# A pool mixer that projects before it pools, more expert tiles transposed ahead, and another order of their loads

## The chip, the cores and the metric

One NeuronCore of a Trainium2 chip runs the whole program. The metric is device time in microseconds (us). TensorE is PE (its weight loads are PEld), VectorE is DVE, ScalarE is ACT, GpSimd is POOL and SyncE is SP. All DMAs of this kernel but the row gathers are issued from SP's queue, in order.

## The reference

The input is `x`, 512 tokens of 1024 features, fp32. Two blocks follow one another.

The first block is a pool mixer with a residual and a layer norm. Cut to what matters:

```
h = x @ w_in;  u, z = split(h)                    # 2048 columns each
for g, w in enumerate((2, 4, 8, 16)):             # 4 groups of 512 columns
    m[g] = (sum of the last w rows of u[g]) / min(t + 1, w) - u[g]
    m[g] = (m[g] @ w_grp[g]) * scale[g]
x = layer_norm(2**0.25 * x + (m * silu(z)) @ w_out)
```

Pooling runs along the tokens, and the projection `w_in` along the features, so either may come first.

The second block has a modulation vector `ada = silu(c) @ w_ada`, a mixer of short convolutions and a linear recurrence (LRU), and PEER, a mixture of 16384 experts: each token picks 8 x 16 experts by key scores, and the result is the sum of `coef * expert_v[i]` with `coef = g * gelu(expert_u[i] . h)`.

## The kernel before, in words

**Precision.** Matrices are split into a high and a low fp32r part (`split`, L107: ACT copies the high part, DVE or POOL subtracts for the low one). A product is three matmuls (`mm3`, L137). `wload` (L121) loads 512 KB of weights into a ring of three buffers and splits them.

**Pool mixer (0 to some 375 us).** `x` is transposed on PE, split into `xh` and `xl`, and POOL adds the two back to `xT` (L209). For each of four groups, `x_group` (L232) pools the columns of `xT` on DVE by doubling steps (L239), subtracts (L243), mends the first tokens (L245, L246) and splits the result; `m_group` (L250) projects it with `w_in` (4 x 8 x 3 matmuls of 512 columns); `z_group` (L217) projects `xh`, `xl` for the gate; `gate_group` (L263) applies `w_grp`, scale and gate; `y_group` (L311) applies `w_out` and adds into `ya`. The last group's tail is `last_group` (L281), in which a tile of 128 tokens goes on to the layer norm as soon as it is done. Beside that, `ada` (L334) computes the modulation on DVE from 96 loads of 256 KB, and `ada_fin` (L345) sums it over partitions on PE. The list `AF_` says at which point of a group that is done.

**Convolutions and LRU (375 to 612 us).** 20 weight tiles; between them `pre_u` (L541) transposes tiles of `expert_u` ahead of time: one tile of 128 experts is loaded in two halves, each by four DMAs (`u_load`, L531: one for each quarter of the features, into a strip of 32 partitions), each half is transposed on DVE (L539) and stored to DRAM (`ut_d`, L551). `NU` = 20 tiles are made so, one after each of 16 chunks and four at the end.

**PEER.** The first 128 tokens take their experts by row gathers (L1180, POOL's queue), the other 384 take all 128 tiles of 128 experts densely. `stage_a` (L869) brings tile i of `expert_u` into transposed form and multiplies it with the tokens (24 matmuls of 384 columns):

- i below `NU`: load the finished transpose (L890), split (L893, L894);
- i from `NU` to 37: load the plain tile, transpose it on PE (8 transposes, L881), split out of PSUM (L883, L885);
- i from 38 on: `u_load` in quarters of 128 KB into the ring of weight buffers, transpose on DVE (2 us, L539), split.

Tiles up to 37 run before the dense loop, most of them among the G stage (750 to 951 us), in which one-hot products (L1134) turn the chosen experts into a dense matrix. In the dense loop (some 960 to 1990 us, 128 steps) step i multiplies `expert_v` tile i (`stage_v`, L922) and makes `stage_a(i + 11)`; from step 27 on the gathers run at about 2.5 of 512 KB a step, spread by step number (L1214), and DVE consumes them (L1192, L1203).

The order on each engine and queue is set by the framework's planner (L1290): it lists what is ready by its own model, in the order of the program where it has a choice, so loads and DVE work of a later line can come before waiting work of an earlier one.

## Time and profile before

| | us |
|---|---|
| median of 3 runs (lowest, highest) | 2038.66 (2033.51, 2040.03) |
| the profiled execution: its own time | 2042.83 |
| its span, first to last instruction | 2041.0 |
| PE busy in it | 1822.1 |
| DVE busy in it | 1787.4 |

The page of the profile gives busy time by engine, the span in slices, and the chain of waits that ended last. The view by stretches gives the same for any stage; the groups by line give what each kind of instruction took and what its engine waited for before it; the DMA view gives packets, bytes and the time that packets took. A busy PE is not PE at its peak, since the ends of matmuls are modelled.

### The profile page before, as it was taken

Reading aid. Unit: us, or ns where it says so; the run is one execution under the profiler, and the core shown is the slowest. Engines: PE = TensorE matmul, PEld = TensorE weight load, DVE = VectorE, ACT = ScalarE, POOL = GpSimd, SP = SyncE. Lnnn points to the kernel's source line nnn. Section 1 sums busy time; section 2 is a strip of 40 time slices with the busy share of each in tenths; the row PEclk is TensorE's granted clock in tenths of the full one; section 3 lists DMA queues with packets and bytes.
Section 4 is the critical chain, followed back from the end, with each engine's and each line's share of the span. In section 5 each row is a group of like instructions: output and inputs, shape, how many; then the busy total and the mean of one; then the engine's idle time right before and its main releaser. Section 6 shows DMA issues by size and latency. Waiting matters only on the chain.

```text
span 2041.0 us, 26681 instructions
## 1 busy us (share of the span) xinstructions
PE 1822.1 (89%) x9003; PEld 1586.7 (78%) x9003; DVE 1787.4 (88%) x3088; ACT 827.9 (41%) x1318; POOL 727.3 (36%) x492
## 2 busy tenths in 40 slices
PE   8999889887899968888988899899898998989897
PEld 6787667765699968888777788788787887878886
DVE  8989887989869999896998898899898898989856
ACT  4433333445453359987333232233232232232334
POOL 3113222333340000000245555455555565656424
PEclk9999999998899979999999899999999999999999
DMA  5545583565463325547869999999999999999932
GB/s 166 181 150 151 167 267 107 150 211 178 146 188 97 103 65 207 191 160 251 265 225 288 265 295 262 291 282 291 274 278 276 300 284 282 298 263 293 286 116 97
DMA packets 288293, 441.13 MB, mean 216 GB/s; under 512 B 24600, under 2 KB 203652, under 8 KB 285084
## 3 DMA queue, kind: packets, MB, share of 16 engines
q1 hardware_dynamic: 251292, 305.19, 49.6%
q0 software_dynamic: 36864, 134.23, 21.3%
q8 instruction: 71, 1.16, 0.3%
q14 instruction: 66, 0.54, 0.1%
HBM read 393.11 MB, written 46.23 MB: 215 GB/s over the span
## 4 chain that ended last, share of the span: by engine, by line
DVE 33%; DMA 24%; PE 17%; issue 13%; ACT 5%; POOL 4%; SPq 2%; DVEq 0%; POOLq 0%; ACTq 0%
DMA uraw<-in_expert_u 10%; DMA wraw<-in_expert_v 4%; DMA gu<-in_expert_u,idx 3%; PE bank L140 3%; PE bank L139 3%; PE bank L138 3%; DMA araw<-in_w_ada 2%; DVE wlo L116 2%; DVE ut L539 2%; DVE og L1132 2%; DMA gv<-in_expert_v,idx 2%; DVE junk L1192 2%; DVE sw L239 2%; SPq L534 2%; DVE acc L1203 2%
## 5 line engine op out<-in xcount | busy, mean ns | idle before, releaser
L114 POOL TENSOR_TENSOR wlo<-wraw,whi 128x1024 fp32r<-128x1024 f32 x111 | 290.0, 2614 | 818.3 <-ACT whi L112 799.3
L140 PE MATMUL aux<-h2h,ul 128*128 128x384 f32 x1024 | 368.1, 360 | 75.3 <-DVE ul L116 68.2
L112 ACT ACTIVATE whi<-wraw 128x1024 fp32r<-128x1024 f32 x218 | 229.3, 1055 | 507.3 <-DMA wraw<-in_expert_v 369.4
L138 PE MATMUL aux<-h2h,uh 128*128 128x384 f32 x1024 | 363.9, 355 | 14.8 <-ACT gl L904 5.9
L139 PE MATMUL aux<-h2l,uh 128*128 128x384 f32 x1024 | 360.2, 352 | 0.0
L139 PE MATMUL o<-wlo,wh 128*128 128x512 f32 x756 | 298.1, 394 | 11.0 <-DVE wlo L116 10.6
L138 PE MATMUL o<-whi,wh 128*128 128x512 f32 x756 | 291.3, 394 | 9.5 <-ACT whi L112 9.5
L140 PE MATMUL o<-whi,wl 128*128 128x512 f32 x756 | 296.6, 392 | 0.0
L140 PEld LDWEIGHTS aux<-h2h,ul 128*128 128x128 f32 x1024 | 203.8, 199 | 92.4 <-DVE ul L116 83.8
L539 DVE STREAM_TRANSPOSE ut<-uraw 128x1024 f32<-128x1024 f32 x90 | 195.9, 2176 | 71.1 <-DMA uraw<-in_expert_u 70.1
L1180 POOL DMA_INDIRECT gu<-in_expert_u,idx x128 | 173.9, 1359 | 204.6 <-DVE junk L1192 173.3
L1180 POOL DMA_INDIRECT gv<-in_expert_v,idx x128 | 182.8, 1428 | 153.2 <-DVE acc L1203 111.9
L138 PEld LDWEIGHTS aux<-h2h,uh 128*128 128x128 f32 x1024 | 204.4, 200 | 22.7 <-ACT uh L112 7.9
L139 PEld LDWEIGHTS aux<-h2l,uh 128*128 128x128 f32 x1024 | 203.6, 199 | 3.3
L112 ACT ACTIVATE uh<-ut 128x1024 fp32r<-128x1024 f32 x90 | 94.9, 1054 | 205.1 <-DVE ut L539 193.6
L1192 DVE SCALAR_TENSOR_TENSOR junk<-gu,hrow 128x1024 bf16<-128x1024 f32 x128 | 171.8, 1342 | 5.7 <-DMA gu<-in_expert_u,idx 5.6
L1203 DVE SCALAR_TENSOR_TENSOR acc<-gv,cf,acc 128x1024 f32<-128x1024 f32 x127 | 171.3, 1349 | 5.3 <-DMA gv<-in_expert_v,idx 4.9
L139 PEld LDWEIGHTS o<-wlo,wh 128*128 128x128 f32 x756 | 143.3, 190 | 42.1 <-DVE wlo L116 14.0
L138 PEld LDWEIGHTS o<-whi,wh 128*128 128x128 f32 x756 | 143.3, 190 | 37.1 <-ACT whi L112 10.2
L140 PEld LDWEIGHTS o<-whi,wl 128*128 128x128 f32 x756 | 143.4, 190 | 30.2
L116 DVE TENSOR_TENSOR wlo<-wraw,whi 128x1024 fp32r<-128x1024 f32 x107 | 147.9, 1383 | 7.0 <-ACT whi L112 7.0
L138 PE MATMUL bank<-ah,whi 128*128 128x512 f32 (+1 forms) x320 | 123.0, 389 | 6.0 <-ACT ah L112 4.9
(376 smaller groups left out, 3562.5 us busy)
## 6 DMA issues: line engine op xcount, KB each, us to landing
wraw<-in_expert_v SPq DMA_DIRECT2D x128, 512.0 KB
uraw<-in_expert_u SPq DMA_DIRECT2D x360, 128.0 KB
araw<-in_w_ada SPq DMA_DIRECT2D x96, 256.0 KB
g_d<-gs SPq DMA_DIRECT2D x24, 1024.0 KB
gt<-g_d SPq DMA_DIRECT2D x15, 1536.0 KB
wraw<-in_pool_w_in SPq DMA_DIRECT2D x32, 512.0 KB
wraw<-in_w_in SPq DMA_DIRECT2D x20, 512.0 KB
praw<-in_expert_u SPq DMA_DIRECT2D x160, 64.0 KB
```

The source lines that it names most:

```text
L112: S.activation(hi, src, AF.Copy)
L114: G.tensor_tensor(lo, src, hi.bitcast(F32), op=OP.subtract)
L116: V.tensor_tensor(lo, src, hi.bitcast(F32), op=OP.subtract)
L138: i = PE.matmul(out, lhsT=l[0], rhs=r[0], start=first, stop=False)
L139: PE.matmul(out, lhsT=l[0], rhs=r[1], start=False, stop=False)
L140: PE.matmul(out, lhsT=l[1], rhs=r[0], start=False, stop=last)
L239: V.tensor_tensor(nxt[:, :, step:], cur[:, :, step:], cur[:, :, :T - step], op=OP.add)
L534: nc.sync.dma_start(raw[32 * q:32 * q + 32], U[i * P + a0 * 32:i * P + (a0 + na) * 32, q * 256:(q + 1) * 256].rearrange("(a r) d -> r a d" ...
L539: V.transpose(out=ut.rearrange("p k (a r) -> p a k r", r=32), in_=raw.rearrange("p a (c k) -> p a k c", k=KD))
L1180: G.indirect_dma_start(out=r, out_offset=None, in_=src, in_offset=bass.IndirectOffsetOnAxis(ap=idx[t][:, s:s + 1], axis=0))
L1192: paced(V.scalar_tensor_tensor(junk, r, 1.0, hrow[t], op0=OP.mult, op1=OP.mult, accum_out=cf[t][:, s:s + 1]))
L1203: paced(V.scalar_tensor_tensor(acc[t], r, cf[t][:, s:s + 1], acc[t], op0=OP.mult, op1=OP.add))
```

## The change

- The pool mixer projects first. `u_group` computes `u = x @ w_in` for a group with tokens on partitions (4 banks of PSUM, 4 weight loads, 96 matmuls of 512 columns, as `m_group` had), and ACT and DVE split it. `pooled` then pools on PE: for each of 4 column blocks and 4 token tiles it multiplies `u` with a banded matrix of 128 columns and with the 16 columns that reach in from the token tile before; 1/w is applied as the result leaves PSUM. `bands` builds the matrices once. `x_group`, `m_group` and `xT` go.
- The order is u(g+1), gate(g), z(g+1), pooled(g+1), y(g). `AF_` is now (1, 1, 1).
- `NU` is 56. `pre_u` comes three tiles at a time at three points of a group and one after each of the four rows of `y_group`'s second half: 39 tiles in the pool mixer. After each of the 16 chunks of the convolution stage it makes one more, and one at the end.
- `u_load` issues the quarters in the order 0, 2, 1, 3, for the tiles made ahead and for those of the dense loop.
- So in `stage_a` tiles 20 to 55 load the finished transpose; 56 to 127 go on as before.

```diff
-AF_ = (1, 1, 0, 0)
+AF_ = (1, 1, 1)
-NU = 20
+NU = 56
+NP1 = 3
+BW = P + 16
...
-    for q in range(4):
-        G.tensor_tensor(xT[:, 2 * q:2 * q + 2, :], xh[:, q].bitcast(F32), xl[:, q].bitcast(F32), op=OP.add)
...
+    def bands():
+        wide = xp.tile([P, BW], F32, name="wide")
+        past = xp.tile([P, BW], F32, name="past")
+        G.iota(wide, pattern=[[1, BW]], base=0, channel_multiplier=-1, allow_small_or_imprecise_dtypes=True)
+        V.tensor_scalar(past, wide, 0.0, None, op0=OP.is_ge)
+        for g, w_ in enumerate(WINDOWS):
...
+            V.scalar_tensor_tensor(f, wide, float(w_), past, op0=OP.is_lt, op1=OP.mult)
+            V.scalar_tensor_tensor(f[:, :P], ident, -float(w_), f[:, :P], op0=OP.mult, op1=OP.add)
...
+    def u_group(g):
+
+        bs = [bank() for _ in range(NT)]
+        for kk in range(4):
+            w = wload(w_in[kk * 256:(kk + 1) * 256, g * 512:(g + 1) * 512].rearrange("(k p) c -> p k c", p=P), 2)
+            for t in range(NT):
+                s = slice(t * P, (t + 1) * P)
+                for j in range(2):
+                    x = at(xhl, 2 * kk + j)
+                    mm3(bs[t], (x[0][:, s], x[1][:, s]), (w[0][:, j], w[1][:, j]), kk + j == 0, kk == 3 and j == 1)
...
+        for t in range(NT):
+            split(uh[t // 2][:, t % 2], ul[t // 2][:, t % 2], bs[t])
+        return uh, ul
+
+    def pooled(g, u):
...
+            for t in range(NT):
+                m = (band if t else first)[:, :P]
+                o = b[:, t * P:(t + 1) * P]
+                e = o[:, :16]
+                PE.matmul(o, lhsT=part(t, 0), rhs=m, start=True, stop=False)
+                if t == 0:
+                    PE.matmul(e, lhsT=part(t, 0), rhs=rest, start=False, stop=False)
+                else:
+                    PE.matmul(e, lhsT=part(t - 1, 0), rhs=band[:, P:], start=False, stop=False)
+                    PE.matmul(e, lhsT=part(t - 1, 1), rhs=band[:, P:], start=False, stop=False)
+                PE.matmul(o, lhsT=part(t, 1), rhs=m, start=False, stop=True)
...
+            S.activation(h, b, AF.Copy, scale=1.0 / WINDOWS[g])
+            V.scalar_tensor_tensor(l, b, 1.0 / WINDOWS[g], h.bitcast(F32), op0=OP.mult, op1=OP.subtract)
...
     def u_load(raw, i, a0, na):
 
-        for q in range(4):
+        for q in (0, 2, 1, 3):
             nc.sync.dma_start(raw[32 * q:32 * q + 32],
...
+    u = u_group(0)
     sz = z_group(0)
+    bands()
...
-    xg = act_tiles()
-    list(x_group(0, xg))
...
-    for g in range(4):
-        mhl = m_group(g, xg)
...
+    mhl = pooled(0, u)
+    for g in range(3):
+        pre_u(NP1)
+        u = u_group(g + 1)
+        pre_u(NP1)
         ghl = gate_group(g, mhl, sz)
         if AF_[g] == 1:
             ada_fins()
-        xg = act_tiles()
-        sz = z_group(g + 1, x_group(g + 1, xg))
+        sz = z_group(g + 1)
+        pre_u(NP1)
+        mhl = pooled(g + 1, u)
...
         for _ in y_group(g, ghl):
-            pass
+            pre_u(1)
+    ada_fins()
     p1.close()
```

## Rows read from the trace of the kernel before

**Rows 1.** The page: the chain that ended last, share of the span by engine.
```profile
DVE 33%; DMA 24%; PE 17%; issue 13%; ACT 5%; POOL 4%; SPq 2%; DVEq 0%; POOLq 0%; ACTq 0%
```

**Rows 2.** Stretches: us; PE, PEld, DVE, ACT, POOL busy; clock, DMA share, GB/s.
```profile
0.00:375.00 375.00, 342.08 (x1524) 274.94 (x1525) 335.99 (x453) 139.16 (x225) 101.42 (x106) 0.98 0.53 164
375.00:612.00 237.00, 205.15 (x984) 166.19 (x983) 193.18 (x227) 119.65 (x179) 88.08 (x56) 0.92 0.60 183
750.00:951.00 201.00, 174.83 (x1255) 169.19 (x1256) 178.40 (x533) 189.13 (x362) 0.00 (x0) 0.97 0.50 182
1096.00:1150.00 54.00, 41.76 (x189) 35.87 (x189) 41.55 (x47) 15.75 (x22) 22.77 (x16) 0.91 0.99 274
1150.00:1920.00 770.00, 695.43 (x3296) 622.00 (x3295) 700.80 (x699) 225.47 (x321) 424.15 (x270) 0.95 0.97 283
```

**Rows 3.** The same view: two stretches of 40 us in the pool mixer.
```profile
20.00:60.00 40.00, 34.98 (x155) 27.61 (x154) 39.82 (x48) 18.38 (x30) 13.87 (x5) 1.00 0.38 113
140.00:180.00 40.00, 40.00 (x175) 31.76 (x174) 39.56 (x39) 17.82 (x31) 16.41 (x6) 1.00 0.31 94
```

**Rows 4.** Groups by line, DVE, 0 to 375 us: busy us, mean ns | idle before.
```profile
L239 DVE TENSOR_TENSOR sw<-sw 128x1020 f32<-128x1020 f32 (+2 forms) x24 | 33.6, 1398 | 0.0
L239 DVE TENSOR_TENSOR sw<-xT 128x1022 f32<-128x1022 f32 x16 | 23.8, 1489 | 0.0
L243 DVE SCALAR_TENSOR_TENSOR xe<-sw,xT 128x1024 f32<-128x1024 f32 x16 | 23.6, 1478 | 0.2
L116 DVE TENSOR_TENSOR al<-xe,ah 128x1024 fp32r<-128x1024 f32 x16 | 22.7, 1421 | 0.4 <-ACT ah L112 0.4
...
L116 DVE TENSOR_TENSOR sl<-bank,sh 128x512 fp32r<-128x512 f32 x16 | 10.8, 681 | 4.3 <-ACT sh L112 4.3
```

**Rows 5.** Groups by line, 0 to 620 us: the transposes made ahead.
```profile
L539 DVE STREAM_TRANSPOSE put<-praw 128x512 f32<-128x512 f32 x40 | 46.2, 1158 | 12.9 <-DMA praw<-in_expert_u 12.7
```

**Rows 6.** Timeline of PE (start us, us): 256 columns wide; 128 wide in fp32.
```profile
15.20 0.28 PE L140 MATMUL bank<-xh,wlo 128*128 128x256 f32 x1
15.32 0.28 PE L138 MATMUL bank<-xh,whi 128*128 128x256 f32 x1
...
800.07 2.17 PE L1134 MATMUL bank<-og,o 128*128 128x128 f32 x18
```

**Rows 7.** Groups by line, 750 to 951 us: products with one-hot rows, tile transposes.
```profile
L1134 PE MATMUL bank<-og,o 128*128 128x128 f32 x768 | 100.9, 286 | 19.3 <-ACT o L1098 9.8 <-ACT gs L1135 9.3 <-DVE og L1132 0.2
...
L883 ACT ACTIVATE uh<-aux 128x512 fp32r<-128x512 f32 x32 | 19.1, 613 | 5.1 <-PE aux L881 5.1
L881 PE MATMUL aux<-ident,uraw 128*128 128x128 f32 x120 | 18.0, 277 | 2.9 <-ACT gl L904 2.9
```

**Rows 8.** Instructions of tile ut: ns min/median/max, first and last start us.
```profile
L539 DVE STREAM_TRANSPOSE ut<-uraw x90: 2005/2175/2331, 1096.4 to 1956.8; 128x1024 f32<-128x1024 f32 x90
...
L893 ACT ACTIVATE uh<-ut x20: 1045/1060/1064, 591.1 to 728.4; 128x1024 fp32r<-128x1024 f32 x20
```

**Rows 9.** DMA queues, 1062 to 1096 us: packets, MB, share of 16 engines.
```profile
q1 hardware_dynamic: 3161, 5.59, 48.9%
q0 software_dynamic: 1584, 5.78, 47.7%
```

**Rows 10.** DMA queues, 1150 to 1920 us.
```profile
q0 software_dynamic: 32920, 119.91, 50.6%
q1 hardware_dynamic: 84695, 97.09, 46.4%
```

**Rows 11.** Groups by line, 1150 to 1920 us: who waits in the dense loop.
```profile
L140 PE MATMUL aux<-h2h,ul 128*128 128x384 f32 x631 | 230.2, 365 | 66.0 <-DVE ul L116 66.0
...
L539 DVE STREAM_TRANSPOSE ut<-uraw 128x1024 f32<-128x1024 f32 x79 | 171.9, 2176 | 55.6 <-DMA uraw<-in_expert_u 54.6 <-issue 1.1
```

**Rows 12.** Waits (us in total, times, longest): late weights; SP's queue behind a transpose.
```profile
ACT whi L112 <- DMA wraw<-in_w_in: 18.9, 6, 6.7
...
SPq L551 <- DVE put L539: 41.6, 30, 4.6
```

More of the change, by code (lines that the diff above doesn't have):

```diff
@@ L171, in _body @@
     sm = front2.enter_context(tc.tile_pool(name="sm", bufs=8, side="right"))
-    sp_ = p1.enter_context(tc.tile_pool(name="sp_", bufs=3))
+    up = p1.enter_context(tc.tile_pool(name="up1", bufs=2))
     adp = p1.enter_context(tc.tile_pool(name="adp", bufs=1))
-    xT = xp.tile([P, KD, T], F32, name="xT")
     def act_tiles():
@@ L215, in cv, with z_group @@
         return cols[:, col[name][0] + i:col[name][0] + i + n]
-    def z_group(g, other=()):
+    def z_group(g):
         r = []
         for c in range(4):
-            next(iter(other), None)
             if b_first:
@@ L251, in m_group @@
+    def pooled(g, u):
         r = []
+        band, first, rest = band_[g]
         for c in range(4):
-            w = wcols(w_in, g * 512 + c * P, P)
             b = bank()
-            for k in range(KD):
-                mm3(b, (w[0][:, k], w[1][:, k]), at(xg, k), k == 0, k == KD - 1)
+            part = lambda t, i: u[i][t // 2][:, t % 2, c * P:(c + 1) * P]
+            for t in range(NT):
[9 more added lines that the diff above has]
+                PE.matmul(o, lhsT=part(t, 1), rhs=m, start=False, stop=True)
@@ L358, in ada_fins, with u_load, u_turn, pre_u @@
             ada_fin(j, accs.pop(j))
+    U, W = a["expert_u_2"][0], a["expert_v_2"][0]
+    ut_d = tc.dram_tile([max(1, NU), P, 2, KD * 64], F32, name="ut_d")
+    npre = 0
+    def u_load(raw, i, a0, na):
+        for q in (0, 2, 1, 3):
+            nc.sync.dma_start(raw[32 * q:32 * q + 32],
+                              U[i * P + a0 * 32:i * P + (a0 + na) * 32, q * 256:(q + 1) * 256].rearrange("(a r) d -> r a d", r=32))
+    def u_turn(ut, raw):
+        V.transpose(out=ut.rearrange("p k (a r) -> p a k r", r=32), in_=raw.rearrange("p a (c k) -> p a k c", k=KD))
+    def pre_u(n):
+        nonlocal npre
+        for _ in range(n):
+            if npre < NU:
+                for h in range(2):
+                    raw = up.tile([P, 2, 256], F32, name="praw", tag="praw")
+                    u_load(raw, npre, 2 * h, 2)
+                    ut = up.tile([P, KD, 64], F32, name="put", tag="put")
+                    u_turn(ut, raw)
+                    nc.sync.dma_start(ut_d[npre, :, h], ut.rearrange("p k e -> p (k e)"))
+                npre += 1
+    u = u_group(0)
     sz = z_group(0)
+    bands()
     vin = pers.tile([P, P], F32, name="vin")
```

57 lines of the change are left out of this document (16 added, 41 removed).

## Prediction

> **What bounds the kernel now.** I read the chain that ended last first: DVE, DMA and PE share it, so no engine bounds the whole [rows 1]. So I went on to the stretches [rows 2], and from each to the groups and waits within it.
>
> - Pool mixer, 0 to 375 us: PE 342.1 and DVE 336.0 us busy. Where it runs undisturbed, PE is busy for all of 40 us, with 175 matmuls, 0.229 us each; in the first stretch it idles 5.0 us while DVE is full (39.8 of 40) [rows 3]. DVE pools there. PE is the bound, with DVE close behind and DMA at a share of 0.53.
> - G stage, 750 to 951 us: ACT 189.1 of 201 us, then DVE 178.4, then PE 174.8.
> - Dense loop, 1150 to 1920 us: DMA share 0.97; PE has 695.4 of 770 us, DVE 700.8. DMA is the bound there, and the only stall of PE with a weight is for the low half of U, at the end of the chain load, DVE transpose, ACT copy, DVE subtraction: 66.0 us [rows 11].
>
> **The change, part by part.** The sum is made against the profiled execution's own 2042.8 us, which is 4.2 us above the median of the three runs shown.
>
> *Pooling by bands.* The projection keeps its 96 matmuls and four 512 KB loads a group. `pooled` adds for each of 16 column blocks 8 matmuls of 128 columns and 7 of 16: 128 and 112 in all. The trace has no fp32r matmul that narrow. From below: those of 256 columns start 0.12 us apart, each with its own weight load [rows 6]; 240 x 0.12 = 29 us. From above: the 128-column fp32 products start as 18 records in 2.17 us [rows 6], 0.12 us, and there are 768 records for 3 x 128 tokens [rows 7], two each, so 0.24 us; 240 x 0.24 = 58 us. The wide 128 share the number format with the first row and the width with the second, so I take the middle, 0.18; for the 16-column ones the first row, since little streams behind the weight load: 23 + 13 = 36 us of PE.
>
> What goes from DVE: 33.6 + 23.8 + 23.6 + 22.7 = 103.7 us of sums, differences and splits [rows 4]. What comes: 78 half-tile transposes of 1.158 us [rows 5], 90.3 us; 16 splits of `u` out of PSUM of 0.681 us [rows 4], 10.9; and 37 small instructions for the bands, of at most 144 columns, between 0 and 0.681 us; by width 0.19, 7 us. Net +4.5 us of 336, so DVE doesn't become the bound of a stage that PE stretches. Sixteen more copies lie on ACT, and sixteen larger ones go; with 139 of 375 us busy it hides them, and if it didn't, each would cost what a copy of the G stage takes, 0.6 us [rows 7]. POOL's four sums go, the bands' one index pattern comes: covered, since PE's first product no longer needs either.
>
> Of the 36 us PE gets 5 back: the idle time at 20 to 60 us belonged to pooling ahead of the first projection. Stage: **+31 us**, ends +24 and +58. The later sums for the modulation (`AF_`) and the new place of `pooled` ahead of `y_group` move matmuls within a full PE; I cost them at nothing, covered by the other work of the group; without that cover the last `ada_fins`, now straight ahead of `last_group`, would show up as PE idle before it.
>
> *Loads and stores of 39 more tiles in that stage.* Each is 0.524 MB read and written, ten DMAs on SP. At the rate of the next stage, which does this already (183 GB/s at a share of 0.60, so 305 at full), that is 39 x 1.05 MB / 305 = 134 us of DMA time beside 0.53 x 375 = 199: 333 of some 405. Hidden, but with little to spare (a rival below).
>
> *Convolution stage.* 17 instead of 20 tiles: 6 x 1.158 = 7 us less on DVE, which has 193 of 237 us there. DVE doesn't bind throughout: **-4 us** (0 to -7).
>
> *G stage.* Some 15 tiles there lose their 8 PE transposes, 120 in 18.0 us, and two ACT copies of 0.613 us each become one of 1.060 [rows 7, 8]. ACT binds: 15 x 0.17 = 2.5 us; some of PE's time is on the path where ACT waits for it. **-6 us** (-2 to -21).
>
> *Finished tiles in the dense loop.* 18 of the 90 tiles that DVE transposes there [rows 8] come as rows of 4 KB and skip a DVE step of 2.18 us. The loads stay at 0.524 MB. SP's queue moves 97.09 MB in 46.4% of 16 x 770 us, 17.0 GB/s an engine [rows 10]; before the first quarter-loaded tile is transposed at 1096 us it moved 5.59 MB in 48.9% of 16 x 34 us, 21.0 [rows 8, 9]. At those rates a tile takes 1.93 and 1.56 us: 18 x 0.37 = 7 us. From the side of PE: its wait for the low half, 66.0 us over 79 tiles [rows 11], 0.84 a tile, is 15 us for 18. I take **-13 us**, nearer to PE's, since the first of these tiles also stand in the stretch in which PE does least (41.8 of 54 us at 1096 to 1150 [rows 2]). Ends 0 (DMA stays full and gives nothing back) and -39 (18 x 2.18, if all DVE time were on the path).
>
> *The order of the quarters.* It touches the 72 tiles that are left, in the loop that DMA bounds. The gathers move the same 4 KB rows throughout: 5.78 MB in 47.7% of 16 x 34 us, 22.3 GB/s an engine, before the quarters come [rows 9], and 119.91 MB in 50.6% of 16 x 770, 19.2, among them [rows 10]. So something in the loop slows packets that are not its own, and the quarter loads, each into a strip of 32 partitions, are what is new. No run shows another order. From above: back at 22.3 and 21.0 GB/s, DMA would need 0.506 x 0.14 + 0.464 x 0.19 = 16% less, 122 us; PE's idle time caps that at 770 - 695 = 75. From below: nothing. Above zero in any case? A loss isn't excluded, but the same four loads are issued, so only a small one. I take a third of the cap, **-26 us**, since the old order had the same quarters beside the same gathers and only neighbours change.
>
> The Trainium skill (SBUF - State Buffer, Door 1: The DMA port swizzle) has partitions 0 to 63 on one half of the 16 DMA ports and 64 to 127 on the other. By that rule the old order sends two quarters to one half and then two to the other, and the new one alternates; the slowing of the gathers agrees with such a crowding, and full relief would be the end of the range. The same page (Can I just issue two DMAs to hit both halves?) speaks against the change: two DMAs to the two halves were only 6% faster than one; by that the sum would come out 18 us higher.
>
> **Sum:** 31 - 4 - 6 - 13 - 26 = -18 us; 2042.8 - 18 = 2024.8 in the profiled execution's terms, 4.2 less against the median: **2021 us**. About 0.3%, 6 us, is what a measurement of this kernel can tell from no change.
>
> **The rivals.**
>
> 1. *The order gives nothing.* Each quarter's DMA spreads over all engines and they take turns in one queue, so neighbours hardly meet. For: within one queue SP issues them one after another. Against: the gathers' lost 14%. Then 31 - 4 - 6 - 13 = +8: **2047 us**. By the Trainium skill's rule on two halves (SBUF - State Buffer, named above) it would be this rival, less some 8 us.
> 2. *Weights come late in the pool mixer* (the slower side). SP's queue is in order: every store of a transposed half waits for DVE, 41.6 us for 40 stores in the stage before [rows 12], and the weight loads behind it wait too. With 78 stores, 390 DMAs and a DMA share above 0.8, the ring of three weight buffers runs dry. Price: late weights held ACT 18.9 us over 20 loads in the convolution stage [rows 12], where PE has slack; 0.95 us for each of 56 loads here, where it has none, is 53 us: -18 + 53 = +35, **2074 us**. It decides from 18 us of such waits on. Against: the planner may load weights first, and SP's waits are short (4.6 us the longest) beside 5.5 us of PE work for each weight tile, 24 x 0.229.
> 3. *The order pays in full.* The loop speeds up until PE binds, by 60 of the 75 us: 31 - 4 - 6 - 13 - 60 = -52: **1987 us**. For: DMA's share of 0.97 with both other engines near 0.9. Against: PE's waits are not all for DMA.
>
> **How the numbers follow.** Chances: forecast 0.45, its own range 2005 to 2038; rival 1 0.25; rival 2 0.17; rival 3 0.13. The range reaches down into rival 3 and up past rival 1 into the milder part of rival 2: **1978 to 2060**. Faster by over 0.3%: most of the forecast (0.41), rival 3, and 0.04 of the rest, 0.58. Within 0.3%: 0.03 of the forecast and 0.4 of rival 1, 0.13. Slower: 0.29.
>
> **What would show it.** Right: PE busy some 378 us in the pool mixer and its end near 405 us; the narrow matmuls at 0.12 to 0.24 us; DVE's share there no higher; the G stage shorter by a few us with ACT still first; in the dense loop the gathers above 19.2 GB/s an engine, fewer waits for the low half of U, and the loop some 40 us shorter. Wrong: a loop as long as before with the gathers' rate unchanged (rival 1); PE idle behind late weights, or DMA near 1.0, before 405 us (rival 2).

## The result, and the profile after

The changed kernel takes **2089.81 us** (median of four runs, 2084.67 to 2090.61) against 2036.09 beside it: ratio 1.0262 [1.0228, 1.0296], some 54 us slower where 18 us faster was forecast. The profiled execution has a span of 2088.1 us, 47.1 above that of before.

The first two views say where the time is. The last addition of `last_group` closes the pool mixer; its line's view, with first and last start, before and after:

```profile
L308 DVE TENSOR_TENSOR ya<-ya,bank x8: 666/684/689, 335.3 to 373.0; 128x512 f32<-128x512 f32 x8
```

```profile
L343 DVE TENSOR_TENSOR ya<-ya,bank x8: 669/678/687, 435.1 to 477.8; 128x512 f32<-128x512 f32 x8
```

The gathers of `expert_u` and `expert_v` rows run through the dense loop, so the first `gu` and the last `gv` mark its length. Before:

```profile
L1180 POOL DMA_INDIRECT gu<-in_expert_u,idx x128: 941/1289/4496, 1061.3 to 1863.3; - x128
```

```profile
L1180 POOL DMA_INDIRECT gv<-in_expert_v,idx x128: 939/1288/4892, 1114.2 to 1918.3; - x128
```

After:

```profile
L1216 POOL DMA_INDIRECT gu<-in_expert_u,idx x128: 940/1297/4496, 1167.4 to 1910.0; - x128
```

```profile
L1216 POOL DMA_INDIRECT gv<-in_expert_v,idx x128: 939/1298/4900, 1217.1 to 1965.7; - x128
```

The pool mixer ends 104.8 us later. The loop takes 798.3 us instead of 857.0, 58.7 less. Between them little moves: from the end of the pool mixer to the last addition of the convolution stage 213.7 us (before 216.2), from there to the last one-hot product 364.3 (361.7), to the first gather 111.6 (110.4); behind the last gather 122.4 (122.7). The sum is 104.8 - 2.5 + 2.6 + 1.2 - 58.7 - 0.3 = 47.1.

The stretches after (columns as in [rows 2]): pool mixer, G stage, the start of the loop:

```profile
0.00:478.00 478.00, 399.77 (x1750) 324.20 (x1751) 318.95 (x479) 126.97 (x184) 74.03 (x102) 0.88 0.68 213
856.00:1056.00 200.00, 173.67 (x1168) 166.70 (x1167) 181.48 (x516) 190.14 (x342) 2.51 (x1) 0.93 0.52 190
1250.00:1320.00 70.00, 70.00 (x357) 64.16 (x357) 61.67 (x71) 24.77 (x35) 47.09 (x31) 1.00 0.98 343
```

In the pool mixer PE has 399.8 of 478 us, 78 us idle, where before it had 33 [rows 2]; its granted clock is 0.88 instead of 0.98; and DVE is less busy than before, 319.0 us. No engine is full. Two stretches of 40 us of the same view, to be set beside [rows 3]:

```profile
160.00:200.00 40.00, 31.29 (x125) 24.30 (x124) 22.82 (x24) 7.00 (x7) 5.15 (x3) 0.87 0.64 208
200.00:240.00 40.00, 30.94 (x126) 23.22 (x125) 26.21 (x29) 11.36 (x16) 7.92 (x4) 0.91 0.72 217
```

What is waited for there (total, times, longest): DVE for the loads of the tiles made ahead,

```profile
DVE put L407 <- DMA praw<-in_expert_u: 96.1, 38, 5.8
```

and SP's queue for the transposes, and for a free weight buffer (the last two):

```profile
SPq L419 <- DVE put L407: 51.4, 50, 2.8
SPq L125 <- POOL wlo L116: 40.9, 5, 22.1
...
SPq L125 <- DVE wlo L118: 5.7, 5, 2.3
```

ACT's waits for late weights, which rival 2 prices, are 29.1 us:

```profile
ACT whi L114 <- DMA wraw<-in_pool_w_grp: 13.9, 3, 7.8
ACT whi L114 <- DMA wraw<-in_pool_w_out: 11.2, 3, 5.0
ACT whi L114 <- DMA wraw<-in_pool_w_in: 4.0, 2, 2.7
```

Before, the same three are 13.2 + 9.8 + 1.9 = 24.9 us (0 to 373 us). PE itself waits mostly for DVE: of its idle time the view of waits puts 51.6 us down to DVE, spread over splits and additions, where before it was 16.9, and 19.3 to ACT (8.5).

In the loop the two queues, at 1250 to 1320 us, where only finished tiles come, and at 1320 to 1966 us, among quarters (packets, MB, share, as [rows 9]):

```profile
q0 software_dynamic: 3703, 13.47, 53.1%
q1 hardware_dynamic: 5980, 10.53, 44.8%
```

```profile
q0 software_dynamic: 28754, 104.70, 50.5%
q1 hardware_dynamic: 72200, 81.73, 44.3%
```

That is 13.47 MB in 0.531 x 16 x 70 us, 22.6 GB/s an engine for the gathers, and then 20.1; before it was 19.2 among quarters [rows 10]. PE's wait for the low half of U, by line, stays 0.92 us a tile (61.7 over 535 / 8 = 67), where [rows 11] have 0.84:

```profile
L142 PE MATMUL aux<-h2h,ul 128*128 128x384 f32 x535 | 192.3, 359 | 61.7 <-DVE ul L118 61.7
```

### The profile page after: what moved, and what is told of

Its sections match the earlier page's. It is cut to its first block, busy times and chain, and to the rows that moved or that the text cites. A ratio compares the mean times of both kernels' runs of the same rounds, so it can differ in the third digit from the quotient of the medians.

```text
span 2088.1 us, 27278 instructions
## 1 busy us (share of the span) xinstructions
PE 1853.4 (89%) x9099; PEld 1612.1 (77%) x9099; DVE 1726.6 (83%) x3074; ACT 817.0 (39%) x1260; POOL 715.8 (34%) x488
## 4 chain that ended last, share of the span: by engine, by line
DVE 27%; PE 24%; DMA 24%; issue 10%; ACT 6%; SPq 5%; POOL 3%; DVEq 0%; POOLq 0%; ACTq 0%
DMA praw<-in_expert_u 5%; DMA uraw<-in_expert_u 4%; DMA wraw<-in_expert_v 4%; SPq L402 4%; DMA araw<-in_w_ada 3%; DVE put L407 3%; PE o L141 3%; PE aux L142 3%; PE o L142 3%; PE aux L140 3%; PE aux L141 2%; DVE ut L407 2%; PE o L140 2%; PE bank L141 2%; PE bank L142 2%
## 5 line engine op out<-in xcount | busy, mean ns | idle before, releaser
L116 POOL TENSOR_TENSOR wlo<-wraw,whi 128x1024 fp32r<-128x1024 f32 x110 | 283.8, 2582 | 883.2 <-ACT whi L114 448.0
L142 PE MATMUL aux<-h2h,ul 128*128 128x384 f32 x1024 | 359.7, 352 | 63.0 <-DVE ul L118 62.0
L140 PE MATMUL aux<-h2h,uh 128*128 128x384 f32 x1024 | 355.9, 348 | 2.9 <-ACT uh L929 2.9
L1216 POOL DMA_INDIRECT gv<-in_expert_v,idx x128 | 198.9, 1554 | 135.4 <-DVE acc L1239 85.4
L407 DVE STREAM_TRANSPOSE put<-praw 128x512 f32<-128x512 f32 x112 | 128.9, 1156 | 113.7 <-DMA praw<-in_expert_u 107.6
L1239 DVE SCALAR_TENSOR_TENSOR acc<-gv,cf,acc 128x1024 f32<-128x1024 f32 x127 | 180.7, 1423 | 25.9 <-DMA gv<-in_expert_v,idx 25.9
L1228 DVE SCALAR_TENSOR_TENSOR junk<-gu,hrow 128x1024 bf16<-128x1024 f32 x128 | 183.6, 1434 | 9.0 <-DMA gu<-in_expert_u,idx 8.8
L407 DVE STREAM_TRANSPOSE ut<-uraw 128x1024 f32<-128x1024 f32 x72 | 157.2, 2183 | 35.8 <-DMA uraw<-in_expert_u 34.6
L142 PEld LDWEIGHTS o<-whi,wl 128*128 128x128 f32 x756 | 143.1, 189 | 30.9 <-DVE wl L118 0.3
L118 DVE TENSOR_TENSOR wlo<-wraw,whi 128x1024 fp32r<-128x1024 f32 x108 | 137.4, 1273 | 15.0 <-ACT whi L114 12.8
L1170 PE MATMUL bank<-og,o 128*128 128x128 f32 x768 | 108.2, 298 | 23.0 <-ACT gs L1171 18.9
```

Source lines behind the costliest of these rows:

```text
L116: G.tensor_tensor(lo, src, hi.bitcast(F32), op=OP.subtract)
L118: V.tensor_tensor(lo, src, hi.bitcast(F32), op=OP.subtract)
L140: i = PE.matmul(out, lhsT=l[0], rhs=r[0], start=first, stop=False)
L142: PE.matmul(out, lhsT=l[1], rhs=r[0], start=False, stop=last)
L407: V.transpose(out=ut.rearrange("p k (a r) -> p a k r", r=32), in_=raw.rearrange("p a (c k) -> p a k c", k=KD))
L1170: PE.matmul(b[:, u * P:(u + 1) * P], lhsT=o2[:, tok % 8 + u], rhs=og, start=True, stop=True)
```

## The experiments

Each kernel ran beside the kernel before. The pool mixer's end is the last start of the line shown above; the loop is first `gu` to last `gv`; both are from one profiled execution. The diffs show only the lines that matter. Kernels with the same loop differ by some 10 us (850.6 to 862.5 in four, 791.1 to 800.9 in ten), so a smaller difference of one loop is not read.

| kernel | median us | ratio to before | pool mixer ends | loop |
|---|---|---|---|---|
| before | - | 1 | 373.0 | 857.0 |
| changed | 2089.8 | 1.0262 [1.0228, 1.0296] | 477.8 | 798.3 |
| bands alone | 2078.4 | 1.0223 [1.0120, 1.0326] | 412.1 | 850.6 |
| order alone | 2015.1 | 0.9896 [0.9856, 0.9937] | 367.7 | 835.7 |
| four buffers | 2086.1 | 1.0259 [1.0165, 1.0353] | 474.9 | 800.9 |
| old order | 2112.1 | 1.0382 [1.0285, 1.0479] | 483.1 | 816.7 |
| no loads | 2050.0 | 1.0080 [1.0043, 1.0116] | 439.2 | 792.3 |
| no transposes | 2093.9 | 1.0299 [1.0254, 1.0344] | 487.1 | 794.0 |
| whole tiles | 2051.9 | 1.0090 [1.0056, 1.0125] | 443.7 | 794.9 |
| transposes only | 2056.5 | 1.0096 [1.0063, 1.0128] | 438.2 | 791.1 |
| issues only | 2060.7 | 1.0132 [1.0071, 1.0193] | 447.2 | 793.4 |
| late stores | 2074.3 | 1.0167 [1.0106, 1.0228] | 464.5 | 796.4 |
| no stores | 2070.1 | 1.0143 [1.0080, 1.0206] | 458.2 | 799.0 |
| bands mixed in | 2080.0 | 1.0204 [1.0145, 1.0263] | 410.6 | 862.5 |
| earlier sums | 2068.9 | 1.0185 [1.0131, 1.0239] | 386.1 | 860.0 |
| two repairs | 2032.9 | 0.9977 [0.9947, 1.0007] | 416.1 | 798.3 |
| 20 shifted | 1992.4 | **0.9791 [0.9750, 0.9832]** | 371.0 | 805.2 |
| 28 shifted | 1996.8 | 0.9820 [0.9772, 0.9869] | 369.2 | 779.7 |
| two repairs, 56 shifted | 1997.6 | 0.9815 [0.9751, 0.9879] | 419.1 | 742.3 |

### The parts: bands alone, order alone, and the changed kernel less one thing

**Bands alone** (the changed kernel without tiles ahead in the pool mixer, old order):

```diff
-NU = 56
-NP1 = 3
+NU = 20
+NP1 = 0
...
-        for q in (0, 2, 1, 3):
+        for q in range(4):
...
-            pre_u(1)
+            pass
```

> The projection first and the bands on PE stay; the 39 tiles leave the pool mixer (NU = 20 again, all of them in the convolution stage), and the quarters go in the old order. Theory A (the tiles made ahead set the pace of the pool mixer: load, transpose in DVE's order, store, next load in SP's order, two buffers): the pool mixer ends near 385 us, at most 25 us later than before and some 90 earlier than with the change, dense loop as before, total 2035 to 2060 us. Theory B (the bands themselves cost it: PE's narrow matmuls and the new order of groups): the pool mixer still ends 60 us or more later than before, total over 2095 us.

Measured: the pool mixer ends at 412.1, 39.1 us later than before, between both theories. So of the 104.8 us 39 belong to the bands and what comes with them, and 66 to the 39 tiles. Stretches, before and then bands alone:

```profile
0.00:373.00 373.00, 340.83 (x1514) 273.69 (x1514) 334.10 (x449) 137.33 (x221) 100.92 (x103) 0.98 0.53 165
```

```profile
0.00:412.00 412.00, 376.78 (x1747) 312.31 (x1748) 241.47 (x400) 127.90 (x184) 73.28 (x102) 0.93 0.47 148
120.00:160.00 40.00, 40.00 (x192) 33.85 (x191) 13.59 (x16) 8.27 (x11) 4.77 (x2) 0.91 0.18 54
129.00:135.50 6.50, 6.50 (x24) 5.82 (x25) 1.39 (x2) 1.19 (x2) 0.00 (x0) 0.50 0.21 71
320.00:360.00 40.00, 24.81 (x91) 17.52 (x90) 22.97 (x36) 5.69 (x7) 7.96 (x5) 0.76 0.50 163
```

PE's busy time grows by 376.8 - 340.8 = 36.0 us, the idle time stays (32.2 and 35.2). A run of 60 narrow matmuls, in PE's timeline from the first one to the wide one behind the last (start, us):

```profile
124.02 0.23 PE L284 MATMUL bank<-first,ah 128*128 128x128 f32 x1
...
132.18 0.73 PE L140 MATMUL bank<-whi,sh 128*128 128x512 f32 x1
```

That is 8.16 us, and the four runs take 8.38 + 8.16 + 8.43 + 7.07 = 32.0. In the later part of this run the granted clock is 0.50, the lower of its two levels, with PE busy throughout (the row from 129 us). The bands take idle time away in one place, but idle time came elsewhere: in the last row PE has 24.8 of 40 us.

The same rows say what the 66 us of the tiles are made of: in the changed kernel 1750 matmuls keep PE busy for 399.8 us at a mean clock of 0.88, here 1747 for 376.8 at 0.93. So 23 us are matmuls at a lower clock and 43 idle time.

PE's timeline at that idle time, and SP's:

```profile
348.51 0.77 PE L387 MATMUL aux<-ahl,ones 128*1 128x512 f32 x1
355.18 0.58 PE L140 MATMUL bank<-sh,whi 128*128 128x256 f32 x1 [5.90 <-ACT whi L114]
```

```profile
348.35 1.99 SPq L389 DMA_DIRECT2D ada_d<-araw  x2
350.39 0.95 SPq L125 DMA_DIRECT2D wraw<-in_pool_w_grp  x2
```

The last finish of the modulation's sums ends, PE stands for 5.9 us until the split of `last_group`'s first weight, and SP issued the load of that weight (L125) only behind the last finish's stores (L389). Before, a finish lies in the same part of the stage (322 to 339 us), and PE is busy beside it:

```profile
320.00:350.00 30.00, 29.47 (x174) 25.02 (x173) 22.00 (x44) 10.17 (x20) 11.36 (x8) 1.00 0.20 62
```

**Order alone** (before, with the quarters in the new order):

```diff
-        for q in range(4):
+        for q in (0, 2, 1, 3):
```

> The kernel before with the quarters in the order 0, 2, 1, 3 and nothing else. If the order relieves the DMA engines (it does by the dense loop of the changed kernel, 59 us shorter, of which the 18 finished tiles may be the smaller part): gathers above 19.2 GB/s an engine, dense loop 15 to 30 us shorter, total 2005 to 2022 us. If neighbours in one queue hardly meet: total within 6 us of 2036.

Measured: the loop is 21.3 us shorter, the whole by 1.04%, 21 us (13 to 29). The queues at 1110 to 1891 us:

```profile
q0 software_dynamic: 33945, 123.60, 49.8%
q1 hardware_dynamic: 89391, 101.12, 45.5%
```

An engine moves 123.60 MB / (0.498 x 16 x 781 us) = 19.9 GB/s of gathers and 17.8 of the rest, where [rows 10] had 19.2 and 17.0. The gathers' packets, which the change does not touch, are faster by some 3%. The Trainium skill (SBUF — State Buffer, "Can I just issue two DMAs to hit both halves?") has 6% for two DMAs to two halves over one. The 3 and 5% here are of that size, but the page compares two DMAs with one and not two orders of four, and no run here shows why the order matters.

**Old order** (the changed kernel):

```diff
-        for q in (0, 2, 1, 3):
+        for q in range(4):
```

> The changed kernel with the quarters in the old order 0, 1, 2, 3. If the order is worth 15 to 30 us in the dense loop: total 2100 to 2120 us, the dense loop longer by that and the pool mixer the same. If the order is worth nothing: 2090 us, within 6.

Measured: the loop is 18.4 us longer than the changed kernel's; by the ratios the whole is 1.2% longer, 24 us (with both intervals 4 to 45). The order is worth about the same in both. The gathers show it again: among quarters, at 1330 to 1990 us, they run at 103.98 MB / (0.507 x 16 x 660 us) = 19.4 GB/s an engine here, and at 20.1 in the changed kernel.

**Four buffers** (the tiles ahead have four instead of two):

```diff
-    up = p1.enter_context(tc.tile_pool(name="up1", bufs=2))
+    up = p1.enter_context(tc.tile_pool(name="up1", bufs=4))
```

> The changed kernel with four instead of two buffers for the half tiles made ahead in the pool mixer. Theory A in the form that the round trip of two buffers is the pace: DVE's 96 us of waits for these loads fall below 50, the pool mixer ends at least 40 us earlier, total under 2055 us. Theory A in the form that SP's queue is the pace (382 issues of 0.43 us and its waits in order): under 15 us gained, total 2075 to 2095. Theory C (the DMA engines are full there): no gain either.

Measured: 474.9. More buffers alone are worth 3 us, although with them DVE's waits for the loads fall from 96.1 to 70.2 us and SP's for the transposes from 51.4 to 29.4. So a sum of waits is not a price by itself.

### What the 39 tiles cost in the pool mixer

**No loads:**

```diff
+NPM = 39
...
+    fixed = xp.tile([P, 2, 256], F32, name="fixed")
+    G.memset(fixed, 0.5)
...
-                    raw = up.tile([P, 2, 256], F32, name="praw", tag="praw")
-                    u_load(raw, npre, 2 * h, 2)
+                    if npre < NPM:
+                        raw = fixed
+                    else:
+                        raw = up.tile([P, 2, 256], F32, name="praw", tag="praw")
+                        u_load(raw, npre, 2 * h, 2)
```

> The changed kernel, but the 39 tiles made in the pool mixer transpose one fixed tile: their 312 loads of expert_u (tiles 0 to 38) are left out, the transposes and the stores stay. In the changed kernel the pool mixer ends at 478 us, with the bands alone at 412. Theory A (somebody waits in order for these loads: VectorE for the tile, or SP's queue, which issues them between the weights): the pool mixer ends at 412 to 430 us, and the whole is 40 to 65 us shorter than the changed kernel, about 2025 to 2050. Theory B (the transposes' own 78 x 1.16 us = 90 us of VectorE is what costs): it ends at 455 us or later, and the whole is within 20 us of the changed kernel.

Measured: 439.2, between the two: the loads cost 38.6 us, and 27.1 stay. SP's wait for the transposes in this run (0 to 480 us, 89.4 of it before 440):

```profile
SPq L426 <- DVE put L408: 98.7, 76, 7.0
```

That is nearly twice the wait of the changed kernel, and a run below shows that here it does no harm.

**No transposes:**

```diff
+                    if npre < NPM:
+                        nc.sync.dma_start(ut_d[npre, :, h], raw.rearrange("p a d -> p (a d)"))
+                        continue
```

> The changed kernel, but the 39 tiles made in the pool mixer are stored as they were loaded: their 78 transposes on VectorE are left out, all loads and stores stay, each store now waiting for its load on SP's queue. Theory A1 (VectorE stands in order behind each load, and the evictions behind it come late): the pool mixer ends at 412 to 430 us, the whole 40 to 65 us under the changed kernel. Theory A2 (SP's queue, through its 390 issues and its in-order waits, or the transfers themselves, bring the weights late): it ends at 455 us or later, the whole within 25 us of the changed kernel, or above it.

Measured: 487.1, later by 9. Loads and stores with no DVE work between them still cost 487.1 - 412.1 = 75 us over the bands alone. The run replaces DVE's wait for a landing by SP's, so it shows that the cost doesn't need DVE's wait, and says nothing of SP's.

**Whole tiles** (4 loads of 128 KB and one store instead of 8 of 64 KB and two):

```diff
+                if npre < NPM:
+                    raw = up.tile([P, 4, 256], F32, name="praw", tag="praw")
+                    u_load(raw, npre, 0, 4)
+                    ut = up.tile([P, 2, KD, 64], F32, name="put", tag="put")
+                    for h in range(2):
+                        u_turn(ut[:, h], raw[:, 2 * h:2 * h + 2])
+                    nc.sync.dma_start(ut_d[npre].rearrange("p h d -> p (h d)"), ut.rearrange("p h k e -> p (h k e)"))
+                    npre += 1
+                    continue
```

> The changed kernel, but the 39 tiles of the pool mixer are loaded whole, 4 loads of 128 KB instead of 8 of 64 KB, with one store instead of two: same bytes, same transposes, 195 SP issues instead of 390. Theory A2 in the form that SP's time to issue is the limit (about 0.43 us each, some 85 us fewer): the pool mixer ends 25 us or more earlier, at 453 or before, the whole at 2065 or less. Theory A1 (VectorE waits for a landing) or full DMA queues: it ends within 15 us of 478, the whole within 15 us of the changed kernel.

Measured: 443.7, 34 us earlier at the same bytes. Two stretches of it:

```profile
160.00:200.00 40.00, 35.61 (x146) 28.59 (x146) 27.19 (x29) 9.40 (x11) 7.06 (x3) 0.92 0.99 291
200.00:240.00 40.00, 38.40 (x187) 31.67 (x187) 32.20 (x38) 13.33 (x19) 8.34 (x4) 0.93 1.03 291
```

DMA is at a share of 1 and 291 GB/s, and PE has 35.6 and 38.4 of 40 us; the changed kernel has 0.64 and 0.72, 31.3 and 30.9 in the same two stretches above. So it is the pieces that cost, and not the bytes. (Two buffers of whole tiles hold as much as four of halves; four buffers alone gave 3 us.)

**Transposes only** (the kernel without loads, without its 78 stores too):

```diff
+                    if npre >= NPM:
+                        nc.sync.dma_start(ut_d[npre, :, h], ut.rearrange("p k e -> p (k e)"))
```

> The kernel whose loads of the 39 tiles were left out (its pool mixer ended at 440 us, the bands alone at 412), and their 78 stores left out too, the later reads taking other tiles: what is left of the work ahead in the pool mixer are 78 transposes on VectorE, 90 us, with no transfer and no wait for one. Theory D (the rest of the stage's loss, 28 us, is VectorE's time and its order: the windows of the run without loads show VectorE busy 39.5 of 40 us): it ends at 430 or later, the whole 2040 to 2055. Theory E (the rest is the stores: their 78 issues on SP, in order, behind transposes): it ends at 412 to 422, the whole 2015 to 2030.

Measured: 438.2. So the stores, with all of SP's waits for the transposes, cost 1 us where no loads stand between them, and the transposes cost 26.1. With nothing to wait for, they pile up early:

```profile
40.00:80.00 40.00, 32.92 (x158) 28.28 (x157) 40.00 (x42) 10.37 (x16) 2.42 (x1) 0.84 0.20 66
80.00:120.00 40.00, 31.05 (x122) 24.12 (x121) 40.00 (x59) 9.10 (x13) 5.66 (x2) 0.91 0.46 136
```

DVE is full, 40.00 of 40 us, and PE has 32.9 and 31.1. With the bands alone PE is full in the same stretches and DVE is not:

```profile
40.00:80.00 40.00, 40.00 (x195) 34.38 (x194) 22.71 (x45) 12.30 (x18) 4.87 (x2) 0.91 0.47 152
80.00:120.00 40.00, 40.00 (x177) 32.85 (x176) 28.89 (x48) 16.37 (x21) 6.42 (x3) 1.00 0.65 204
```

**Issues only** (the kernel without loads, with 312 loads of 64-byte runs that nobody reads):

```diff
...
+                        tiny_ = up.tile([P, 2, 16], F32, name="tinyl", tag="tinyl", bufs=8)
+                        for q in (0, 2, 1, 3):
+                            nc.sync.dma_start(tiny_[32 * q:32 * q + 32],
+                                              U[npre * P + 64 * h:npre * P + 64 * h + 64, q * 256:q * 256 + 16].rearrange("(a r) d -> r a d", r=32))
```

> The kernel whose loads of the 39 tiles were left out (they stay left out, the transposes work on one fixed tile; its pool mixer ended at 439 us), with 312 loads that nobody reads put where those loads were: the same number of issues on SP, 64 runs each as before, but of 64 bytes instead of 1 KB, 1.3 MB in all instead of 20.4. Theory A2 (SP's time to issue 312 loads, 0.44 to 0.46 us each, 140 us in order with the weights, is what the loads cost): the pool mixer ends at 465 to 485. Theory J (their bytes, landing times or buffers are): it ends at 436 to 446. Between: both.

Measured: 447.2, 8 us later than without them. SP's timeline (start, us):

```profile
150.85 1.95 SPq L423 DMA_DIRECT2D tinyl<-in_expert_u  x4
152.90 0.37 SPq L430 DMA_DIRECT2D ut_d<-put  x1
153.35 1.81 SPq L423 DMA_DIRECT2D tinyl<-in_expert_u  x4
```

SP is at it here without a pause: four loads in 1.8 to 1.95 us, a store in 0.37. That alone costs little. In the changed kernel the same queue has pauses between them:

```profile
183.09 1.85 SPq L402 DMA_DIRECT2D praw<-in_expert_u  x4
186.84 0.34 SPq L419 DMA_DIRECT2D ut_d<-put  x1
```

**Late stores** (four buffers, each store two halves later):

```diff
+LATE = 2
...
+                    late.append((npre, h, ut))
+                    if npre >= NPM or len(late) > LATE:
+                        store_u()
...
+    def store_u():
+        i, h, ut = late.pop(0)
+        nc.sync.dma_start(ut_d[i, :, h], ut.rearrange("p k e -> p (k e)"))
+
+    late = []
```

> The changed kernel with four buffers instead of two for the tiles made ahead in the pool mixer, and there each half's store issued two halves later, behind the loads of the next two: same loads, transposes, bytes and issues, but SP no longer comes to a store whose transpose is still to run. With all 312 issues but no landing to wait for, the pool mixer ended at 447 us; in the changed kernel at 478, where SP waited 51 us for transposes. Theory K (issues alone cost 8 us, and the other 31 are SP's waits in order for landing and transpose): it ends at 445 to 458. Theory L (the 31 are VectorE's waits in order for the landings, 96 us in the changed kernel, or the transfers): it ends at 468 to 482.

**No stores** (four buffers):

```diff
+                    if npre >= NPM:
+                        nc.sync.dma_start(ut_d[npre, :, h], ut.rearrange("p k e -> p (k e)"))
```

> The changed kernel with four buffers instead of two for the tiles made ahead in the pool mixer and without the 78 stores there (the later reads take other tiles; the stores of the 39 tiles are left out): the loads with their bytes, landings and issues stay, and so do the transposes, but SP waits for none of them except for a free buffer, four halves back. Theory K (SP's waits in order): it ends at 440 to 456. Theory L (VectorE's waits for landings, or the transfers): 465 or later.

Measured: 464.5 and 458.2, between both theories. Taking SP's waits in order away is worth 13 to 20 us, of which the four buffers alone gave 3; the upper figure is from the run that leaves out the stores themselves too. DVE's wait for the landings is still there with late stores:

```profile
DVE put L409 <- DMA praw<-in_expert_u: 75.2, 40, 4.5
```

So the 39 us of the loads go to three: 8 to the issues alone, 13 to 20 to SP standing in order behind transposes while the rest of its queue waits, and the other 11 to 18 to what is left with the pieces, DVE's waits for landings among it. The split is by subtraction, from runs that change more than one wait, and the last part was not split further. Nor is it late weights that are the cost: with late stores ACT waits 50.9 us for them and with whole tiles 46.1, more than in the changed kernel, and both end earlier.

### The bands' other costs

**Bands mixed in** (bands alone, the narrow matmuls of groups 1 to 3 between the gates' chunks):

```diff
-    def z_group(g):
+    def z_group(g, other=()):
...
             S.activation(r[c], b, AF.Silu)
+            next(iter(other), None)
...
-    def pooled(g, u):
+    def pooled(g, u, r):
...
-        return r
+            yield
...
-        sz = z_group(g + 1)
+        mhl = []
+        sz = z_group(g + 1, pooled(g + 1, u, mhl))
```

> The bands alone (20 tiles ahead, old order of quarters; 2078 us, pool mixer ends at 412, TensorE at half clock for 6.8, 6.8, 6.8 and 3.4 us in and behind the four runs of narrow matmuls), but the narrow matmuls of the groups 1 to 3 issued in fours of a c, each after one c of the gates' 512-wide matmuls, instead of all in one run; those of group 0 stay as they are. Theory F (the fall of the clock belongs to a long run of narrow matmuls): the three later falls go, half of 17 us comes back, the pool mixer ends at 402 to 407. Theory G (it belongs to something else, for example the evictions or the stage's rhythm): the falls stay, it ends at 410 to 415.

Measured: the clock stays up, the stretch shown above for bands alone at 0.91 is now

```profile
120.00:160.00 40.00, 40.00 (x191) 33.26 (x190) 12.58 (x14) 8.54 (x10) 4.79 (x2) 1.00 0.25 79
```

and 15 narrow matmuls, a run between wide ones, take 1.62 us, 0.108 each:

```profile
109.16 0.23 PE L283 MATMUL bank<-first,ah 128*128 128x128 f32 x1
...
110.78 0.44 PE L140 MATMUL bank<-xh,whi 128*128 128x512 f32 x1
```

But the pool mixer ends at 410.6, 1.5 us earlier. Theory F has the mechanism, not the price: the last addition of `y_group` starts 3.6 us earlier (337.1 instead of 340.7), `last_group`'s first one 2.5 us later (372.0 instead of 369.5), so by the hole ahead of it the gain is gone.

**Earlier sums** (bands alone, the modulation's sums by six, six, none):

```diff
-        acc = adp.tile([P, 512], F32, name="acc", tag="acc", bufs=4)
+        acc = adp.tile([P, 512], F32, name="acc", tag="acc", bufs=6)
...
-        for j in range(4 * g, 4 * g + 4):
+        for j in range(6 * g, min(6 * g + 6, 12)):
```

> The bands alone, but six sums of the modulation instead of four behind each of the groups 0 and 1, none behind group 2, with six buffers for them: the last finish comes in group 2, and nothing stands between the last y_group and last_group. In the kernel with the bands alone TensorE has a hole of 6 us there and half the clock for 17 us. Theory H (the hole and the clock are the price of the last finish, whose cover, m_group(3), went with the change): the hole goes, the pool mixer ends at 396 to 404. Theory I (last_group's weights come late by themselves): within 4 us of 412.

Measured: 386.1, 26 us earlier, more than expected. The whole stage and the place of the hole:

```profile
0.00:386.00 386.00, 368.86 (x1731) 307.15 (x1732) 239.84 (x399) 127.58 (x184) 73.11 (x98) 0.95 0.50 157
320.00:360.00 40.00, 40.00 (x214) 34.19 (x213) 22.34 (x41) 11.99 (x15) 4.82 (x2) 1.00 0.42 133
```

PE is busy for 40.00 of 40 us at full clock where it had 24.8 at 0.76. The whole gains less: the loop of this execution is 9 us longer, and the medians, 2068.9 and 2078.4, don't differ beyond their intervals. The kernel before was not run with the sums moved so. What is left of the bands is 386.1 - 373.0 = 13 us: PE has 28 us more work than before and 15 us less idle time.

**Two repairs** (the changed kernel with the diffs of whole tiles and of earlier sums):

> The changed kernel with two of the causes taken out: the 39 tiles loaded whole (195 issues instead of 390; alone this ended the pool mixer 34 us earlier) and six sums of the modulation behind each of the first two groups (alone 26 us earlier with the bands alone). If the causes stand for themselves the gains add up: the pool mixer ends at 412 to 422, the whole at 2022 to 2038. If both fill the same hole of TensorE: it ends at 432 to 444, the whole 2045 to 2055.

Measured: 416.1, 62 us earlier than the changed kernel; singly they gave 34 and 26. The costs add up. The whole is 0.9977 [0.9947, 1.0007] of the kernel before, 1.1% under whole tiles alone, so here the earlier sums show in the whole too, with some 23 us.

### The finished tiles in the loop

**20 shifted** (order alone, and the 20 tiles made ahead are 38 to 57):

```diff
+N0 = 38
...
-                    u_load(raw, npre, 2 * h, 2)
+                    u_load(raw, N0 + npre, 2 * h, 2)
...
-        ty = 4 if i < NU else ATY if i < RT else 2
+        ty = 4 if N0 <= i < N0 + NU else ATY if i < RT else 2
```

> The kernel before with the quarters in the order 0, 2, 1, 3 (2015 us as measured), but the 20 tiles that are made ahead are numbers 38 to 57 instead of 0 to 19, so that all of them are read finished in the dense loop and tiles 0 to 37 take their turn on TensorE as the code already has it. The finished tiles pay more in the dense loop than ahead of it: in the changed kernel 18 of them went with some 35 us. Theory 1 (they pay inside the loop, 1.5 to 2 us each, because their 4 KB packets move faster and they take no transposes there): the loop is 30 to 40 us shorter than with the order alone, the stage ahead up to 24 us longer, the whole 1985 to 2010. Theory 2 (they do not pay by themselves, the changed kernel's loop gained from something else): 2015 or more.

Measured: the loop 30.5 us shorter than with the order alone, the first gather 14 us later, the whole 0.9791, **the lowest median of the study** and faster than the kernel before and the order alone. The 175 us from the first gather on, order alone and then 20 shifted:

```profile
1058.00:1233.00 175.00, 157.38 (x733) 136.44 (x732) 158.83 (x167) 53.01 (x74) 93.60 (x63) 0.96 0.93 288
```

```profile
1070.00:1245.00 175.00, 174.44 (x857) 155.43 (x856) 155.91 (x183) 63.60 (x87) 118.27 (x79) 1.00 0.97 348
```

With finished tiles PE is all but full (174.4 of 175 us) and DMA moves 348 GB/s; with quarters PE has 157.4 and DMA 288, at nearly the same share. So packets move faster where finished tiles come than where quarters come. Whether it is the quarters' runs of 1 KB, their strips of 32 partitions or their number, no run separates.

**28 shifted** (`NU = 28` in it):

> The kernel with the tiles 38 to 57 made ahead (1992 us), with 8 more, 28 in all (38 to 65). The eight are made at the end of the conv stage, where VectorE was busy 31.6 of 50 us and the DMA share was 0.28: 8 x 2 x 1.16 = 18.6 us of VectorE. Theory 1 (a finished tile is worth 1.5 to 2 us in the dense loop): the loop is 12 to 16 us shorter, the conv stage 0 to 12 us longer, the whole 1976 to 1992. Theory 2 (the loop has had its gain, another bound has taken over): the loop within 5 us, the whole 1990 or more.

Measured: the loop is 25.5 us shorter again, more than theory 1 has, but the first gather comes 11 us later, and the medians, 1996.8 and 1992.4, don't differ beyond their intervals. The whole gained nothing that shows.

**Two repairs, 56 shifted:**

> The kernel with whole loads and the earlier sums (2033 us), with the 56 tiles made ahead being numbers 38 to 93 instead of 0 to 55: all 56 are then read finished in the dense loop, and tiles 0 to 37 take their turn on TensorE ahead of it. By the runs with 20 and 28 shifted tiles and the 18 of the changed kernel a finished tile is worth 1.5 to 2.1 us of the loop, and the tiles on TensorE cost 14 us ahead of it: 2033 + 14 - 38 x 1.5 to 2.1 = 1967 to 1990. If the loop has no more to gain than with 28 finished tiles (780 us): 2033 + 14 - 18 = 2029 or more.

Measured: 38 more finished tiles make the loop 56 us shorter, 1.5 us each, the whole 35 us shorter than with the repairs alone. That misses both ranges of the whole: of the loop's gain 11 us go to a later first gather and 8 to a longer tail behind the last one. The loop's first 310 us:

```profile
1100.00:1410.00 310.00, 306.01 (x1498) 272.71 (x1496) 271.45 (x315) 109.11 (x151) 194.94 (x126) 0.99 0.93 331
```

PE is the bound there, with 306.0 of 310 us. This ends level with 28 shifted tiles and the old pool mixer.

## Why the prediction was wrong

**The failing step is the 39 tiles in the pool mixer,** "Hidden, but with little to spare". It counted DMA time, and that held: 0.68 x 478 = 325 us for the 333 forecast, and whole tiles bring the same bytes at a share of 1 and end 34 us earlier. What the sum put at nothing is SP's queue and the order on it (rival 2 named both), and DVE's order. 312 loads of some 0.46 us are 144 us of issues, and the waits stand between them; SP's spare time, its wait for a free weight buffer, falls from 110.7 + 84.9 us with the bands alone

```profile
SPq L125 <- DVE wlo L118: 110.7, 33, 18.2
SPq L125 <- POOL wlo L116: 84.9, 15, 22.1
```

to 40.9 + 5.7. Measured cost: 39 us. How it reaches PE is known in part: PE's added idle time is put down to DVE above all, and 11 to 18 of the 39 us stay unsplit. The Trainium skill (DMA: Bandwidth & Descriptors, Rules for kernel authors) says to coalesce small transfers and counts those under 64 KB as mostly overhead. These are 64 KB each, at that limit and not under it; the 34 us for twice the size agree with the advice to coalesce.

**DVE.** "Net +4.5 us, so DVE doesn't become the bound": the sum was high rather than low (318 to 319 us busy against 334 before; it left out the mends of the first tokens, L245 and L246, some 12 us that go too), but a sum over 478 us says nothing of when. The transposes alone cost 26 us, because they fill DVE for stretches in which PE needs its splits.

**Bands.** 36 us forecast and 36.0 more busy time measured, but that is luck. At full clock the narrow matmuls start 0.108 us apart in the mean, under the 0.12 of the lower end; 240 are 26 us. With the bands alone they take 32.0, as the clock falls within each run, and the other 4 are other matmuls. The sum had no term for the clock. The net term, +31, is 39 in the run with the bands alone. Of these 26 come from the edit costed at nothing, `AF_` and the last `ada_fins` (with the sums that it finishes, which the run moved too): the text named the place and what it would show, and gave it no price. Before, PE was busy beside that finish, 29.5 of 30 us, with `m_group(3)` in the program there. Without it the bands cost 13, below the lower end of 24, since PE's busy time grows by 28 us and its idle time shrinks by 15 and not by 5.

**Convolution and G stage.** -2.5 us measured for -4. The -6 us of the G stage did not come: that stretch is 2.6 us longer, and ACT still is the first there with 190 of 200 us; why is open.

**Finished tiles.** -13 forecast. The changed kernel's loop is 37 us under that with the order alone, and old order 34 under bands alone: about 2 us each for 18; 1.5 for the shifted ones. The size was wrong because the step took only the tile's own queue and PE's wait, while the gathers gain too: 22.6 GB/s an engine without quarters and 20.1 among them. The prediction had seen that slowing, and used it for the order alone. An estimate from the rows of 20 shifted: what 348 GB/s move in 175 us takes 36 us more at 288, and 30.5 were measured.

**Order.** -26 forecast; -21 us and some -24 measured. Right, with the gathers above 19.2 as the text asked, and rival 1 falls with it, as does rival 3. The size, a third of a cap, had no row behind it; that it came so near is luck.

**Rival 2** came out on the right side (2074 forecast, 2090 measured) and named the right queue, but the nearness of the number is luck. Its price, 53 us of ACT's waits for late weights, did not come: they are 29.1 us against 24.9 before. Its mechanism is a part of the cost: SP's waits behind transposes are worth 13 to 20 us of the 39, and 98.7 us of such waits cost 1 us where no loads stand between.

By its own steps the sum is 13 + 26 (bands, uncovered finish) + 26 + 39 (transposes, loads) = 104 for the pool mixer against 31, then -59 for the loop against -39, and about +1 against -10 between them: some +46 against the -18 forecast, and the spans differ by 47. That it closes shows nothing, as the parts are differences along one row of runs; that the costs add is shown by two repairs.

## What to carry to other kernels

Work that is moved into a full stage is to be priced on every queue that it passes, by its number of pieces and not by its bytes: here half the pieces gave back 34 of 39 us. If a stage's order changes, ask for each small tail (a finish, a store) what covered it before and what covers it now; here a finish without its cover was worth 26 us of the stage. And work prepared ahead is worth most where it takes slow transfers out of a stage that DMA bounds: the same 20 tiles, numbered so that the loop reads them, took the kernel from 0.9896 to 0.9791 of the one before.

## What the hardware showed that was not expected

PE's granted clock falls to the lower of its levels (1.2 instead of 2.4 GHz) in runs of narrow matmuls with no idle time: with the bands alone PE is busy for 6.50 of 6.50 us at 129.0 to 135.5 us, in and behind a run of 60, and the clock is 0.50; with the same matmuls in runs of 15 between wide ones it is 1.00. The order in which four loads of one tile are issued changes the speed of packets of another queue: 19.2 to 19.9 GB/s an engine for the gathers, and 19.4 to 20.1 in the changed kernel.
